# Redividing SBUF and the eight PSUM banks of an fp32r encoder kernel, and giving one more low part per product set to accumulating DMAs

## The chip, the cores and the metric

The kernel runs on one core of a Trainium2 chip. The metric is the device time of one execution in microseconds (us). Five compute queues matter below: PE (TensorE, matrix products), DVE (VectorE), ACT (ScalarE), POOL (GpSimd) and SP (SyncE, which here only starts DMAs). POOL also starts DMAs of its own, among them accumulating ones.

## The reference

The computation is a two-layer encoder on x of 512 tokens by 1024 features. Cut to what matters:

```python
for i in range(DEPTH):                       # DEPTH = 2, ALPHA = 4 ** 0.25
    x = layer_norm(ALPHA * x + 0.5 * swiglu(x, w_gate[i, 0], w_up[i, 0], w_down[i, 0]))
    y = mixer_ab(x) if i % 2 == 0 else mixer_c(x)   # attention of several kinds
    x = layer_norm(ALPHA * x + y)
    x = layer_norm(ALPHA * x + memory_attn(x, mem))  # 4 heads into 256 memory tokens
    x = layer_norm(ALPHA * x + 0.5 * swiglu(x, w_gate[i, 1], w_up[i, 1], w_down[i, 1]))

def swiglu(x, w_gate, w_up, w_down):         # hidden width 2816
    return (silu(x @ w_gate) * (x @ w_up)) @ w_down
```

`mixer_ab` is 8 dense heads with 2-D rotary (A) and 8 heads in a band of +-128 tokens with a sink logit (B). `mixer_c` is 16 heads of clamped neighbourhood attention with a learned bias, worked in 8 pairs.

## The kernel before

**Stages.** `run()` goes through FFN 0, mixer_ab, memory 0, FFN 1, FFN 2, mixer_c, memory 1, FFN 3. In the profiled execution the FFNs lie at about 0–370, 760–1100, 1100–1445 and 1840–2191 us, mixer_ab at 370–560, mixer_c at 1445–1680, and the two memory stages behind the mixers.

**Arithmetic.** Each fp32 operand is split into a high part (an ACT cast to fp32r) and a low part (raw minus high, a DVE subtract), and `mm3` makes three matmuls of them: high·high, high·low, low·high. `wide(raw, shape, added)` splits a 128x1024 weight tile. With `added`, no DVE instruction is used: ACT writes `-raw` in fp32r into the low tile, and a DMA from POOL's queue adds `raw` to it in place.

**FFN.** A Strassen-like scheme of 7 products (1 to 7) replaces 8. `hidden()` computes 512 hidden columns by the products 1, 2, 6, 5, 7, 3, 4 of 24 matmuls of 256 columns each, into three banks pa, pb, pc with copies of pa and pc in between (v, u, y); products 1, 2 and 4 take a block of the weights as it is, the others sums and differences of blocks that DVE makes. It is called 10 times per FFN, 40 in all. `ADDED` lists the products whose left low part comes by the accumulating DMA. `down_fast()` (DF) multiplies two hidden blocks with the down weights, again by 7 products of 12 matmuls (2 banks x 2 x 3): product 1 into two banks, then 6, 2, 5, 7, 3, 4. Each bank is evicted by a DVE SCALAR_TENSOR_TENSOR of 128x512 into x or into the slab u2. Product 2 goes on in product 1's banks and 3 in those of 5, 4 in those of 7, so product 2 cannot start before the evictions of product 1.

**Order.** `Graph.record` notes every instruction (which is why the profile gives line 141 for all of them), and `Graph.emit` schedules them itself by a table of costs: each engine takes the first ready instruction by program order. A tile of a tag is granted in program order out of that tag's buffers (`grant`): a later tile never passes an earlier one of its tag that still waits for a buffer. So the number of buffers of a tag sets how far ahead work can be moved, and every engine then runs what it was given strictly in order.

**Pools.** `slab` is 4 KB per partition (weights, their high and low parts), `t2` 2 KB (attention probabilities, temporary mixes), `x` the residual. The PSUM has 8 banks of 2 KB: tag `a` 3 (hidden, scores), `d` 2 (DF products 1, 2, 7, 4; projections, attention outputs) and `t` 3 (transposes; DF 6, 5, 3). Two tiles stand apart: `junk`, the unused output of the Square in `layer_norm`, and `band`, the mask of the band heads. In tile names the digits are running numbers.

## Time and profile before

| what | us |
|---|---|
| median of three runs | 2192.2 (2191.91 to 2193.2) |
| the profiled execution itself | 2192.96 |
| its span, first to last instruction | 2191.2 |
| PE busy | 2142.4 (98%) |
| DVE busy | 1756.9 (80%) |
| ACT busy | 1155.9 (53%) |
| POOL busy | 318.1 (15%) |

The span is 1.76 us shorter than the execution's time, and the execution's time is 0.76 above the median. "Busy" of PE counts overlapping matmuls as one stretch. The granted TensorE clock is 0.997 over the span. An "idle before" or a "wait" in the profile is a stretch in which an engine had nothing running, with what ended it. Timelines show the start, the duration and the engine of a run of like instructions, in which xN stands for N of them.

### The profile page before, as it was taken

What the parts mean: (1) busy time and instruction counts of PE and PEld (TensorE: products, weight loads), DVE (VectorE), ACT (ScalarE), POOL (GpSimd) and SP (SyncE); (2) the same over time, 40 slices, a digit from 0 to 9 for tenths busy, and PEclk for the clock granted to TensorE, in tenths of its full rate; (3) what the DMA queues carried; (4) which work ended last, traced back from release to release, by engine and by line L of the source; (5) the groups of instructions that cost most, each with busy time, mean ns of one, the idle gap of its engine ahead of it and who ended that gap; (6) DMA issues with size and microseconds to landing.
All of it is one profiled execution on the core that took longest, in us unless ns stands there. A gap on an engine that the chain in (4) does not pass through costs nothing.

```text
span 2191.2 us, 35698 instructions
## 1 busy us (share of the span) xinstructions
PE 2142.4 (98%) x14212; PEld 1959.0 (89%) x14212; DVE 1756.9 (80%) x2476; ACT 1155.9 (53%) x1754; POOL 318.1 (15%) x431
## 2 busy tenths in 40 slices
PE   8999999999999999999999999999999999999998
PEld 8899998778898899998999998998889988999997
DVE  6989987778855799999799999767777458999985
ACT  6555554466533455654565555445554335655552
POOL 0000202534000000002000002113420000000020
PEclk9999999999999999999999999999999999999999
DMA  6544463011533164555435554635555233454453
GB/s 178 152 119 135 135 181 125 0 30 52 163 104 116 58 187 120 139 141 146 144 93 140 144 154 131 182 95 152 140 159 158 92 106 87 131 149 132 127 148 95
DMA packets 190199, 276.12 MB, mean 126 GB/s; under 512 B 11216, under 2 KB 141904, under 8 KB 190032
## 3 DMA queue, kind: packets, MB, share of 16 engines
q1 hardware_dynamic: 175440, 221.40, 32.7%
q0 software_dynamic: 14592, 52.44, 12.3%
q8 instruction: 111, 1.82, 0.3%
q14 instruction: 56, 0.46, 0.1%
HBM read 217.17 MB, written 4.19 MB: 101 GB/s over the span
## 4 chain that ended last, share of the span: by engine, by line
PE 85%; DVE 11%; ACT 2%; issue 1%; POOL 1%; DMA 0%; POOLq 0%; ACTq 0%; DVEq 0%
PE a L141 48%; PE d L141 26%; PE t L141 10%; DVE slab L141 8%; DVE t L141 2%; ACT slab L141 1%; DMA slab<-slab 0%; POOL t L141 0%; DVE x L141 0%; ACT t L141 0%; POOL rms8y L141 0%; POOL rms2y L141 0%; POOL slab L141 0%; DVE xl L141 0%; DVE mn L141 0%
## 5 line engine op out<-in xcount | busy, mean ns | idle before, releaser
L141 DVE TENSOR_TENSOR slab<-slab,slab 128x1024 fp32r<-128x1024 f32 (+2 forms) x776 | 920.0, 1217 | 58.0 <-ACT slab L141 54.8
L141 ACT CAST slab<-slab 128x1024 fp32r<-128x1024 f32 (+1 forms) x616 | 609.9, 1021 | 296.4 <-DVE slab L141 184.2
L141 PE MATMUL d<-slab,slab 128*128 128x512 f32 (+2 forms) x2432 | 576.2, 384 | 15.8 <-DVE slab L141 11.7
L141 PE MATMUL a<-xh,slab 128*128 128x256 f32 (+1 forms) x2960 | 571.5, 290 | 1.8 <-ACT slab L141 1.4
L141 PE MATMUL a<-slab,slab 128*128 128x256 f32 (+2 forms) x4216 | 555.9, 288 | 8.4 <-ACT t L141 6.1
L141 PEld LDWEIGHTS a<-slab,slab 128*128 128x128 f32 x4216 | 527.6, 192 | 22.2 <-ACT t L141 8.4
L141 PEld LDWEIGHTS d<-slab,slab 128*128 128x128 f32 x2432 | 438.9, 188 | 103.6 <-DVE slab L141 17.3
L141 PEld LDWEIGHTS a<-xh,slab 128*128 128x128 f32 x2960 | 474.1, 192 | 13.5 <-ACT slab L141 3.1
L141 PE MATMUL a<-xl,slab 128*128 128x256 f32 (+1 forms) x1480 | 428.3, 290 | 0.0
L141 PEld LDWEIGHTS a<-xl,slab 128*128 128x128 f32 x1480 | 283.5, 192 | 4.3
L141 POOL DMA_DIRECT2D slab<-slab x80 | 69.3, 866 | 1065.1 <-ACT slab L141 725.5
L141 DVE SCALAR_TENSOR_TENSOR x<-d,x 128x512 f32<-128x512 f32 x216 | 148.2, 688 | 56.0 <-PE d L141 54.2
L141 ACT CAST slab<-t 128x512 fp32r<-128x512 f32 (+1 forms) x209 | 109.8, 564 | 89.3 <-PE t L141 64.4
L141 PE MATMUL t<-slab,slab 128*128 128x512 f32 (+1 forms) x648 | 151.3, 381 | 1.8 <-DVE slab L141 1.7
L141 PEld LDWEIGHTS t<-slab,slab 128*128 128x128 f32 x648 | 115.1, 188 | 28.8 <-DVE slab L141 4.4
L141 DVE TENSOR_TENSOR slab<-t,slab 128x512 fp32r<-128x512 f32 (+1 forms) x209 | 128.3, 647 | 14.2 <-ACT slab L141 13.5
L141 POOL TENSOR_TENSOR t<-t,l 128x256 f32<-128x256 f32 (+2 forms) x104 | 84.5, 831 | 351.5 <-DVE l L141 292.4
L141 DVE TENSOR_TENSOR t<-a,t 128x512 f32<-128x512 f32 (+1 forms) x121 | 83.4, 689 | 64.0 <-PE a L141 57.1
L141 ACT ACTIVATE t<-t 128x512 f32<-128x512 f32 x80 | 50.6, 633 | 147.5 <-DVE t L141 147.5
L141 ACT COPY t<-a 128x512 f32<-128x512 f32 x120 | 69.9, 586 | 83.3 <-PE a L141 82.6
L141 PE MATMUL a<-slab,xh 128*128 128x256 f32 (+1 forms) x432 | 98.5, 321 | 3.8 <-ACT slab L141 3.1
L141 ACT ACTIVATE slab<-slab 128x1024 fp32r<-128x1024 f32 x80 | 84.6, 1057 | 0.0
(109 smaller groups left out, 1898.6 us busy)
## 6 DMA issues: line engine op xcount, KB each, us to landing
slab<-ffn_w_gate SPq DMA_DIRECT2D x88, 512.0 KB
slab<-ffn_w_up SPq DMA_DIRECT2D x88, 512.0 KB
slab<-ffn_w_down SPq DMA_DIRECT2D x88, 512.0 KB
slab<-slab POOLq DMA_DIRECT2D x80, 512.0 KB, 5.7
slab<-mem_w_kv SPq DMA_DIRECT2D x32, 512.0 KB
slab<-c_w_in SPq DMA_DIRECT2D x24, 512.0 KB
slab<-t SPq DMA_DIRECT2D x96, 128.0 KB
slab<-mem_w_q SPq DMA_DIRECT2D x16, 512.0 KB
```

The lines of the kernel that those rows point to most:

```text
L141: op.call = lambda: fn(*args, **kw)
```

## The change

1. `ADDED` gains product 1: in each of the 40 `hidden()` calls a third low part comes by ACT and an accumulating DMA of 512 KB instead of a DVE subtract.
2. `t2` goes from 14 buffers of 2 KB to 8. `junk` (2 KB) becomes a t2 tile in each layer_norm, `band` (1.5 KB) a t2 tile that lives through mixer_ab. `slab` goes from 31 to 35 buffers (16 KB more).
3. The eight banks become two sets: `d` 3, and `u` 5 for what was `a` and `t`.
4. Small tiles have 6 buffers in place of 8.

```diff
-ADDED = (2, 4)
+ADDED = (1, 2, 4)
...
-    BUFS = {"t2": 14, "slab": 31, "a": 3, "d": 2, "t": 3}
+    BUFS = {"t2": 8, "slab": 35, "u": 5, "d": 3}
...
     def ps(self, tag):
-        return self.tile(self.psp, [P, 512], F32, tag)
-
-    def small(self, n, tag, bufs=8):
+        return self.tile(self.psp, [P, 512], F32, "d" if tag == "d" else "u")
+
+    def small(self, n, tag, bufs=6):
...
-        nc.scalar.activation(self.junk, x, AF.Square, bias=nmu, scale=1.0, accum_out=var)
+        nc.scalar.activation(self.t2(BF16, (P, D)), x, AF.Square, bias=nmu, scale=1.0, accum_out=var)
...
+        band = self.t2(F32)[:, :384]
+        nc.sync.dma_start(out=band, in_=a["band"])
         nsink = self.small(8, "nsink", 1)
```

The pools decide the order, so the diff doesn't show what moves. Three places follow; rows are instructions in an engine's own order, x2 two alike.

PE at the end of a group of FFN 1, before: d_1816 holds product 1 and then product 2 of down_fast, t_1818 and t_1819 product 6, t_1820 product 5, and a_1846 is product 1 of the next `hidden()`.

```order
L141 MATMUL t_1819<-slab_1797,slab_1796 128x512
L141 MATMUL t_1820<-slab_1804,slab_1803 128x512 x2
L141 MATMUL t_1820<-slab_1805,slab_1803 128x512
L141 MATMUL t_1820<-slab_1804,slab_1803 128x512
L141 MATMUL a_1846<-xh_80,slab_1830 128x256
L141 MATMUL a_1846<-xl_81,slab_1830 128x256
L141 MATMUL a_1846<-xh_80,slab_1830 128x256
L141 MATMUL a_1846<-xl_81,slab_1830 128x256
L141 MATMUL d_1816<-slab_1801,slab_1799 128x512
```

The same place after: d_1827 holds products 1 and 2, u_1829 and u_1830 product 6, u_1831 and u_1832 the two banks of product 5.

```order
L141 MATMUL u_1830<-slab_1808,slab_1807 128x512
L141 MATMUL u_1831<-slab_1815,slab_1814 128x512
L141 MATMUL u_1832<-slab_1815,slab_1814 128x512
L141 MATMUL u_1832<-slab_1816,slab_1814 128x512
L141 MATMUL u_1832<-slab_1815,slab_1814 128x512 x2
L141 MATMUL u_1832<-slab_1816,slab_1814 128x512
L141 MATMUL d_1827<-slab_1812,slab_1810 128x512
```

Ahead of product 2 now stand 5 of the 6 matmuls of product 5's second bank, which had no bank before, and the four matmuls of the next `hidden()` are gone from there: its product 1 begins only behind product 4 of down_fast.

DVE at that place, before, from the last mix of `hidden()` that reads PSUM (a_1779) to the evictions of product 1 (d_1816, d_1817).

```order
L141 TENSOR_TENSOR slab_1732<-a_1779,t_1704_1782 128x512
L141 TENSOR_TENSOR t_1717_1795<-t_1716_1794,slab_1731 128x512
L141 TENSOR_TENSOR t_1732_1810<-slab_1732,t_1717_1795 128x512
L141 TENSOR_TENSOR slab_1800<-slab_1732,slab_1799 128x1024
L141 TENSOR_TENSOR slab_1796<-t_1717_1795,slab_1796 128x512
L141 TENSOR_TENSOR slab_1803<-t_1716_1794,slab_1803 128x512
L141 TENSOR_TENSOR slab_1811<-t_1732_1810,slab_1811 128x512
L141 TENSOR_TENSOR slab_1813<-slab_1787,slab_1812 128x1024
L141 TENSOR_TENSOR slab_1815<-slab_1788,slab_1814 128x1024
L141 SCALAR_TENSOR_TENSOR slab_1613<-d_1816,slab_1613 128x512
L141 SCALAR_TENSOR_TENSOR slab_1613<-d_1817,slab_1613 128x512
```

The same place after, from the same mix (u_1790) to the evictions of d_1827 and d_1828.

```order
L141 TENSOR_TENSOR slab_1743<-u_1790,t_1715_1793 128x512
L141 TENSOR_TENSOR t_1728_1806<-t_1727_1805,slab_1742 128x512
L141 TENSOR_TENSOR slab_1814<-t_1727_1805,slab_1814 128x512
L141 TENSOR_TENSOR slab_1811<-slab_1743,slab_1810 128x1024
L141 TENSOR_TENSOR slab_1807<-t_1728_1806,slab_1807 128x512
L141 TENSOR_TENSOR t_1743_1821<-slab_1743,t_1728_1806 128x512
L141 TENSOR_TENSOR slab_1826<-slab_1799,slab_1825 128x1024
L141 TENSOR_TENSOR slab_1822<-t_1743_1821,slab_1822 128x512
L141 SCALAR_TENSOR_TENSOR slab_1624<-d_1827,slab_1624 128x512
L141 SCALAR_TENSOR_TENSOR slab_1624<-d_1828,slab_1624 128x512
```

One of the three 128x1024 subtracts no longer stands between the mix and the evictions; it is done further ahead.

ACT in the band heads of mixer_ab, before: `CAST slab<-t` is the high part of a head's turned probabilities, `CAST slab<-d` that of an attention output, `ACTIVATE t<-t,mn` the exponentials of the next head's four token tiles.

```order
L141 CAST slab_1055<-t_1054 128x384
L141 ACTIVATE t_981_1059,l_1061<-t_981_1059,mn_1060 128x257
L141 CAST slab_1057<-t_1056 128x256
L141 CAST slab_1108<-slab_1107 128x1024
L141 CAST slab_1074<-d_1048 128x512
L141 ACTIVATE t_985_1063,l_1065<-t_985_1063,mn_1064 128x385
L141 ACTIVATE t_989_1067,l_1069<-t_989_1067,mn_1068 128x385
L141 ACTIVATE t_993_1071,l_1073<-t_993_1071,mn_1072 128x257
```

The same place after.

```order
L141 CAST slab_1058<-u_1057 128x384
L141 CAST slab_1060<-u_1059 128x256
L141 ACTIVATE t_984_1062,l_1064<-t_984_1062,mn_1063 128x257
L141 ACTIVATE t_988_1066,l_1068<-t_988_1066,mn_1067 128x385
L141 CAST slab_1077<-d_1051 128x512
L141 ACTIVATE t_992_1070,l_1072<-t_992_1070,mn_1071 128x385
L141 ACTIVATE t_996_1074,l_1076<-t_996_1074,mn_1075 128x257
```

The first exponential of the next head now stands behind all of a head's casts of turned probabilities, since a t2 buffer comes free for it only then.

## Prediction

> **What bounds the kernel now.** I read the page first: busy times, then the chain of work that ended last (row 2: shares of the span by engine), then the stretches by stage, then PE's waits, then timelines of two stalls.

> ```profile
> PE 2142.4 (98%) x14212; PEld 1959.0 (89%) x14212; DVE 1756.9 (80%) x2476; ACT 1155.9 (53%) x1754; POOL 318.1 (15%) x431
> PE 85%; DVE 11%; ACT 2%; issue 1%; POOL 1%; DMA 0%; POOLq 0%; ACTq 0%; DVEq 0%
> ```

> PE is the bound, with DVE in the chain for a ninth of it. The change alters no matmul, so its gain can only come from the time in which PE waits. The stretches (window, length, busy us of each engine, then granted clock, DMA share and GB/s) say where that is:

> ```profile
> 50.00:85.00 35.00, 31.59 (x176) 26.28 (x176) 33.64 (x42) 18.60 (x23) 0.85 (x1) 1.00 0.43 114
> 85.00:370.00 285.00, 281.23 (x1955) 262.41 (x1955) 248.49 (x293) 156.96 (x195) 38.54 (x39) 1.00 0.52 143
> 408.00:560.00 152.00, 140.39 (x787) 116.39 (x786) 122.21 (x319) 98.48 (x240) 65.75 (x104) 1.00 0.17 42
> 760.00:1100.00 340.00, 335.76 (x2356) 314.13 (x2355) 300.32 (x352) 190.11 (x240) 31.42 (x31) 1.00 0.53 143
> 1100.00:1445.00 345.00, 342.04 (x2410) 320.37 (x2409) 305.81 (x358) 193.49 (x244) 39.72 (x46) 1.00 0.51 138
> 1445.00:1680.00 235.00, 233.68 (x1484) 209.85 (x1484) 168.93 (x351) 123.42 (x271) 65.12 (x122) 1.00 0.53 147
> 1840.00:2140.00 300.00, 296.22 (x2113) 278.89 (x2112) 271.65 (x305) 174.01 (x216) 30.51 (x29) 1.00 0.51 133
> 2140.00:2191.00 51.00, 40.33 (x251) 36.22 (x249) 27.88 (x45) 13.25 (x20) 2.21 (x4) 0.93 0.27 86
> ```

> PE's idle time, length minus busy: 3.8 + 4.2 + 3.0 + 3.8 = 14.8 us in the four long FFN stretches, 3.4 in 50–85 (FFN 0's first groups), 11.6 in mixer_ab, 1.3 in mixer_c, 10.7 in the tail. In the FFNs DVE is busy 87 to 91% (300.32 of 340), so there it is the near second. PE's waits by releaser (total us, times, longest), first for the whole span, then for mixer_ab alone (408–560):

> ```profile
> PE d L141 <- DVE slab L141: 11.7, 18, 1.4
> PE a L141 <- ACT t L141: 6.1, 6, 1.2
> ...
> PE t L141 <- DVE slab L141: 2.9, 3, 1.3
> PE a L141 <- DVE slab L141: 2.8, 8, 0.7
> ...
> PE a L141 <- DMA slab<-slab: 0.3, 1, 0.3
> ...
> PE d L141 <- DVE slab L141: 2.0, 3, 1.4
> PE a L141 <- ACT t L141: 0.9, 1, 0.9
> ```

> So outside mixer_ab 15 waits of PE's `d` banks for DVE make 9.7 us, and 5 of bank a for ACT 5.2: together 14.9, against 14.8 us idle in the four FFN stretches.

> **The d wait.** Timeline of FFN 1, end of a group; the first row is product 1 of down_fast, the last its product 2:

> ```profile
> 918.98 2.91 PE L141 MATMUL d<-slab,slab 128*128 128x512 f32 x12
> 919.37 0.68 DVE L141 TENSOR_TENSOR slab<-a,t 128x512 f32<-128x512 f32 x1
> ...
> 921.76 4.46 PE L141 MATMUL t<-slab,slab 128*128 128x512 f32 x18
> ...
> 922.65 1.05 ACT L141 CAST slab<-slab 128x1024 fp32r<-128x1024 f32 x1
> ...
> 924.24 2.35 DVE L141 TENSOR_TENSOR slab<-slab,slab 128x1024 fp32r<-128x1024 f32 x2
> ...
> 926.05 0.28 PE L141 MATMUL a<-xh,slab 128*128 128x256 f32 x1
> ...
> 926.40 0.28 PE L141 MATMUL a<-xl,slab 128*128 128x256 f32 x1
> 926.51 1.28 DVE L141 SCALAR_TENSOR_TENSOR slab<-d,slab 128x512 f32<-128x512 f32 x2
> ...
> 927.25 0.96 PE L141 MATMUL d<-slab,slab 128*128 128x512 f32 x3 [0.57 <-DVE slab L141]
> ```

> Product 1's banks were full at about 921.9, but DVE evicts them at 926.51, behind two 128x1024 subtracts at 924.24. PE runs out at 926.40 + 0.12 (four 256-wide matmuls start 0.12 apart) = 926.52 and starts again at 927.25. From start to start that costs 0.73, where the idle column says 0.57: 0.16 more each, because a matmul's shown time overlaps the next.

> *What it costs after.* By the changed order DVE has two such subtracts rather than three between the mix at 919.37 and the eviction: (926.51 - 924.24) / 2 = 1.14 us less. PE has five more 512-wide matmuls of product 5 ahead of product 2 (18 take 926.05 - 921.76 = 4.29, 0.238 each: 1.19 us) and loses the four small ones (926.52 - 926.05 = 0.47): 0.72 more cover. 1.14 + 0.72 - 0.73 = 1.1 us of slack. This is where the third `d` bank, the five `u` banks and product 1's DMA act together: without either the stall shrinks but stays. The 15 waits cost 9.7 + 15 x 0.16 = 12.1 us. Their longest anywhere is 1.4, more than half over my example's 0.57, and not every group has its order, so I take -10; ends 0 and -12.1.

> **The a wait.** FFN 0, hidden block 8:

> ```profile
> 270.50 7.44 DVE L141 TENSOR_TENSOR slab<-slab,slab 128x1024 fp32r<-128x1024 f32 x5
> 277.85 0.68 DVE L141 TENSOR_TENSOR t<-a,t 128x512 f32<-128x512 f32 x1
> ...
> 278.57 0.63 ACT L141 ACTIVATE t<-t 128x512 f32<-128x512 f32 x1
> 279.10 1.06 ACT L141 COPY t<-a 128x512 f32<-128x512 f32 x2
> 279.72 1.46 PE L141 MATMUL a<-slab,slab 128*128 128x256 f32 x10 [1.23 <-ACT t L141]
> ```

> Product 7 waits for the copy of its bank, which stands on ACT behind the silu, which waits for a mix on DVE behind five slab operations. After, two or three stand there, as product 1's subtract (1.2) is gone, and the copies stay in the same ACT order. It has to come 1.4 earlier (1.23 + 0.16). Four such waits and one more: 5.2 + 5 x 0.16 = 6.0; I take -4, ends 0 and -6.

> **What product 1 costs elsewhere.** The groups by shape, the POOL issue's minimum/median/maximum in ns, the landing of all DMAs of POOL's queue into slabs, and the queue's share:

> ```profile
> L141 DVE TENSOR_TENSOR slab<-slab,slab 128x1024 fp32r<-128x1024 f32 x496 | 607.7, 1243 | 50.6 <-ACT slab L141 50.4
> L141 ACT ACTIVATE slab<-slab 128x1024 fp32r<-128x1024 f32 x80 | 84.6, 1057 | 0.0
> L141 POOL DMA_DIRECT2D slab<-slab x80: 850/860/1033, 30.8 to 2133.5; - x80
> DMA to landing us min/median/max: 4.0/5.7/12.2
> q0 software_dynamic: 14592, 52.44, 12.3%
> ```

> Removed: 40 DVE subtracts x 1.243 = 50 us, DVE 80% to 78%. Added: 40 x 1.057 = 42 us on ACT (53 to 55%, 190.11 of 340 in the FFN, so there is room), 40 x 0.866 = 35 us on POOL (idle in the FFNs), and half as many accumulates again: about 12.3% x 40 x 0.5 MB / 52.44 MB = 5% of the DMA engines, whose share in the FFNs is 0.52. No queue nears its end: 0. The DMAs stand in POOL's queue ahead of the tensor_tensors that add u2 to x, which are few.

> What matters is whether the low part lands ahead of product 1. In the changed order its ACT instruction follows two casts behind the point of the CAST at 922.65 above; done, if nothing waits, by 922.65 + 1.05 + 1.05 + 1.06 = 925.8. With 0.87 for the issue and 5.7 to land: 932.4. Product 1 of the next hidden block starts only behind down_fast's 84 matmuls, 918.98 + 84 x 0.238 = 939.0. That is 6.6 us of room, 0.1 with the longest landing of 12.2. The 80 DMAs of products 2 and 4 held PE for 0.3 us in all. I count 0, with up to 3 us for FFN 0's first group, where 3.4 us are idle anyway. Without this cover, a landing 2 us late at 36 blocks would be +72; nothing in the rows comes near.

> [...]

> **mixer_ab and mixer_c.** t2 falls from 14 buffers to 8, of which band takes one through mixer_ab. Rows by shape in 408–560:

> ```profile
> L141 POOL TENSOR_TENSOR t<-t,l 128x384 f32<-128x384 f32 x16 | 14.9, 946 | 3.1 <-DVE l L141 3.0
> L141 ACT ACTIVATE t<-t,mn 128x385 f32<-128x385 f32 x16 | 9.8, 613 | 0.7 <-DVE l L141 0.7
> L141 DVE CUSTOM_DVE_ANT_0 t<-a,band,nsink 128x384 f32<-128x384 f32 x16 | 9.3, 612 | 0.0
> ```

> After, a band head's last two probability tiles get their buffers only when the head before has been transposed. From there to their own transposes: band operation 0.61, exponential 0.61, scaling on POOL 0.95 twice (it does them one after the other), and about 0.8 of small steps and hand-overs by my estimate: 4 us. Between lies, by my count of the changed order's rows, 5.5 us of PE work (the attention output and the next scores); the stretch has 140.39 / 16 = 8.8 us of PE per head. So there is slack of 1.5: 0 lost. Bounds: the whole chain uncovered is 8 heads x 4 = +32; the 11.6 us of idle gone is the other end. On the other side `d` 3 lets the output projection fill PE while a head waits, and five `u` banks let a fourth scores bank start. I take -3 of the 11.6, the d and a waits quoted above for this stretch (2.0 + 0.9).

> In mixer_c the pairs share 8 t2 tiles where an iteration uses 13, so a pair's bias can be fetched only when the pair before is transposed:

> ```profile
> t<-bias POOLq DMA_DIRECT2D x16, 128.0 KB, 3.2
> ```

> Seven pairs x 0 to 3.2 us: 0 to +22. Its stretch has 1.3 us idle now; the rows between leave the bias about as much time as it needs, so I take 0.3 per pair, +2.

> **Four more slabs, six small tiles, junk in t2:** slabs let loads start earlier; SP's loads gave no PE wait outside the first 50 us, so 0. `junk` is held for one ACT instruction per token tile in layer_norm, when few other t2 tiles are alive: 0. The start and the tail (10.7) depend on the same last layer_norm: 0.

> **Sum:** -10 - 4 - 3 + 2 = -15, and -2 of the 2.9 + 2.8 us of other waits for DVE's slab operations, as DVE has 50 us less to do: -17. The profiled execution's own time is 2192.96 (span 2191.2 + 1.76), 0.76 above the median of 2192.2: 2192.96 - 17 = 2176, against the median 2175.

> **Rivals.** (A) *t2 is too small*: in mixer_ab and mixer_c the probabilities' FIFO becomes the bound. For it: 14 buffers to 6 or 7; POOL's scaling is serial, and mixer_ab waits already. Against: 1.5 us of slack. From 1.5 us more of chain per head it starts to cost; at 2 us per band head and 1.5 per pair it gives 2176 + 3 (mixer_ab's gain gone) + 16 + 8.5 (10.5 in place of 2), about 2204; with mixer_c as forecast it passes 2192 from 1.6 us per head on. That is the slower side. Chance 0.10. (B) *The stalls only move*: in DF the eviction of a later product waits, as DVE still has 88% of its time, or product 1's low lands 2 us late in some 7 of the 40 blocks, which eats 14 of the 17. For it: DVE's share in the FFNs falls only by 3 points. Against: the slack of 1.1 and 6.6 above. Then 2185 to 2198, about 2190. Chance 0.14, half of it within 0.2%. (C) *More*: with free banks, mixer_ab's 11.6 us of idle goes by half as well and every FFN wait vanishes: 12.1 + 6 + 8 + 2 = 28, about 2165. Chance 0.12. (D) the forecast, 2168 to 2186: 0.64.

> **How the numbers follow.** 0.2% is 4.4 us, about what a measurement of this kernel can tell from no change: faster means under 2187.8, slower over 2196.6. Faster: D and C, and a third of B: 0.64 + 0.12 + 0.05 = 0.81. Same: 0.07 of B and 0.03 of A: 0.10. Slower: 0.09. The range leaves out most of A, some of B and of C: 2160 to 2191.

> **What would show it.** Right: no d wait of PE for DVE over 0.3 us in the FFNs, idle there under 6 us in the four stretches; the DVE subtract group with 456 of 496; 120 accumulates with a landing under 8 us median; mixer_ab's stretch no longer than 150. Wrong: PE waiting on the slab DMA at product 1, PE idle in 1445–1680 well over 1.3, or waits of DVE's band operation or of the bias for a t2 tile.

## The result and the profile after

| | us |
|---|---|
| before, median of 4 runs | 2192.27 (2191.91 to 2193.2) |
| after, median of 4 runs | 2159.77 (2158.54 to 2161.68) |
| ratio after / before | 0.9852, 95% interval 0.9835 to 0.9869 |
| profiled execution after, and its span | 2161.68, 2159.8 |

The change saves 32.5 us by the medians, 31.4 by the spans of the two profiled executions. The direction was forecast; the size was not: 17 were expected, and the time lies 0.2 us below the range.

The page after, busy times and the chain by engine:

```profile
PE 2130.8 (99%) x14212; PEld 1964.5 (91%) x14212; DVE 1704.2 (79%) x2436; ACT 1190.8 (55%) x1794; POOL 353.4 (16%) x471
PE 91%; DVE 5%; issue 1%; DMA 1%; POOL 1%; ACT 1%; POOLq 0%; DVEq 0%; ACTq 0%
```

DVE's share of the chain falls from 11% to 5%. PE has the same 14212 matmuls, yet its busy time falls by 11.6 us: part of a short wait is counted as busy, because a matmul's shown time reaches over the start of the next (at 256 columns 0.28 us are shown and the next starts 0.12 later, at 512 0.39 and 0.23). The stretches after, in the columns of before (later ones hold slightly other work, since everything has moved up):

```profile
50.00:85.00 35.00, 31.42 (x177) 27.58 (x176) 29.22 (x36) 17.34 (x22) 2.56 (x3) 0.95 0.59 151
85.00:370.00 285.00, 284.49 (x1976) 266.33 (x1976) 244.34 (x290) 166.98 (x206) 42.91 (x46) 1.00 0.60 161
408.00:560.00 152.00, 146.79 (x818) 124.84 (x819) 126.26 (x321) 100.47 (x243) 64.65 (x103) 0.99 0.23 64
760.00:1100.00 340.00, 339.43 (x2402) 319.91 (x2401) 293.89 (x347) 202.10 (x254) 40.88 (x42) 1.00 0.61 160
1100.00:1445.00 345.00, 344.22 (x2441) 324.43 (x2440) 290.90 (x346) 198.18 (x248) 46.79 (x49) 1.00 0.57 150
1445.00:1680.00 235.00, 235.00 (x1508) 213.26 (x1507) 167.03 (x357) 126.07 (x280) 62.99 (x126) 1.00 0.55 157
1840.00:2140.00 300.00, 299.23 (x2104) 281.74 (x2104) 253.53 (x293) 171.26 (x210) 36.78 (x36) 1.00 0.58 147
```

PE's idle time in the four long FFN stretches is 0.5 + 0.6 + 0.8 + 0.8 = 2.7 us where it was 14.8, and 0 in the mixer_c stretch. PE's waits over the whole span, in the columns of before:

```profile
PE u L141 <- ACT slab L141: 3.6, 2, 3.1
PE u L141 <- POOL slab L141: 3.2, 1, 3.2
PE u L141 <- DMA slab<-slab: 3.1, 1, 3.1
PE d L141 <- ACT slab L141: 2.6, 5, 0.5
PE u L141 <- ACT t L141: 2.3, 4, 0.9
PE d L141 <- DVE slab L141: 2.0, 3, 1.3
```

The d waits for DVE fall from 11.7 us (18) to 2.0 (3): the 15 outside mixer_ab are gone. New are single waits of 3 us: one for a low part by DMA, one for POOL. At the end of the group whose stall was shown before:

```profile
905.41 2.91 PE L141 MATMUL d<-slab,slab 128*128 128x512 f32 x12
905.80 0.68 DVE L141 TENSOR_TENSOR slab<-u,t 128x512 f32<-128x512 f32 x1
...
908.15 5.38 PE L141 MATMUL u<-slab,slab 128*128 128x512 f32 x23
...
911.68 1.28 DVE L141 SCALAR_TENSOR_TENSOR slab<-d,slab 128x512 f32<-128x512 f32 x2
```

From the mix to the eviction DVE takes 911.68 - 905.80 = 5.9 us, 926.51 - 919.37 = 7.1 before. Product 2's first matmul starts at 913.37, right behind the 23 matmuls of products 6 and 5. It needs only the first of the two evictions (before, it started at 927.25, while the second one ran until 927.79). That one ends at 912.37: no wait, and 1.0 us to spare.

**A measure for the comparisons.** Idle time undercounts waits, so I use *excess*: the sum, over PE's matmuls in order, of the start-to-start interval less the bare one of its width (0.109 us for 128 columns, 0.120 for 256, 0.174 for 384, 0.227 for 512, about 0.11 for the 64 matmuls of 192: the intervals of the undisturbed rows). All kernels here issue the same matmuls, 2112.2 us of bare intervals, so excess, put to the stage of the earlier matmul, adds up to the difference in PE's last start. "Start" is groups 0 and 1 of FFN 0, "blocks 1–3" the groups with down_fast elsewhere, "blocks 8–10" the FFNs' remaining hidden blocks, "tail" is from PE's last start to the end of the span. In us, from one profiled execution each:

| kernel | start | blocks 1–3 | blocks 8–10 | mixer_ab | memory | mixer_c | tail |
|---|---|---|---|---|---|---|---|
| before | 15.0 | 13.6 | 9.2 | 20.0 | 4.7 | 3.8 | 11.25 |
| only_added | 14.2 | 12.2 | 5.9 | 23.5 | 4.7 | 4.2 | 9.68 |
| only_banks | 13.4 | 1.8 | 24.4 | 11.9 | 0.4 | 2.4 | 11.32 |
| only_pools | 12.9 | 5.4 | 8.0 | 26.3 | 4.7 | 4.1 | 11.26 |
| all_but_added | 10.2 | 1.3 | 14.7 | 14.3 | 0.6 | 0.8 | 11.25 |
| all_but_banks | 14.3 | 1.7 | 3.1 | 26.2 | 4.8 | 4.3 | 9.69 |
| all_but_pools | 13.1 | 1.0 | 25.3 | 12.7 | 0.5 | 2.3 | 9.76 |
| after | 14.8 | 0.5 | 4.1 | 15.5 | 0.6 | 1.0 | 9.70 |
| products_2_4_5 | 9.4 | 0.6 | 15.1 | 15.4 | 0.6 | 0.9 | 9.98 |
| second_block_by_dve | 11.3 | 0.5 | 4.3 | 14.2 | 0.6 | 0.8 | 9.70 |
| u6_d2 | 13.1 | 1.4 | 3.2 | 18.8 | 3.8 | 2.3 | 9.69 |
| u4_d4 | 12.4 | 0.5 | 5.4 | 21.3 | 4.3 | 10.6 | 9.69 |
| t2_10_slab_34 | 11.5 | 0.5 | 3.9 | 10.5 | 0.6 | 6.5 | 9.69 |
| keys_earlier | 9.9 | 0.5 | 4.0 | 14.6 | 0.7 | 0.8 | 9.70 |

Before to after: -0.2, -13.1, -5.1, -4.5, -4.1, -2.8, -1.6, in all -31.4, the difference of the spans.

Each row also holds the stretches of 3.4 us in which PE ran at half rate in that execution (last section); one adds 1.4 to 1.9 us. In mixer_ab there is none in before, all_but_added, second_block_by_dve, t2_10_slab_34 and keys_earlier, two in only_pools, all_but_banks and all_but_pools, and one in each of the others. Blocks 8–10 hold three in only_banks, all_but_added and all_but_pools and two in products_2_4_5.

### The profile page after: what moved, and what is told of

Its sections match the earlier page's. It is cut to its first block, busy times and chain, and to the rows that moved or that the text cites. A ratio compares the mean times of both kernels' runs of the same rounds, so it can differ in the third digit from the quotient of the medians.

```text
span 2159.8 us, 35839 instructions
## 1 busy us (share of the span) xinstructions
PE 2130.8 (99%) x14212; PEld 1964.5 (91%) x14212; DVE 1704.2 (79%) x2436; ACT 1190.8 (55%) x1794; POOL 353.4 (16%) x471
## 4 chain that ended last, share of the span: by engine, by line
PE 91%; DVE 5%; issue 1%; DMA 1%; POOL 1%; ACT 1%; POOLq 0%; DVEq 0%; ACTq 0%
PE u L141 62%; PE d L141 28%; DVE slab L141 3%; DMA slab<-slab 1%; DVE t L141 1%; POOL x L141 0%; DVE x L141 0%; ACT slab L141 0%; DVE mn L141 0%; ACT t L141 0%; POOL slab L141 0%; POOL rms8y L141 0%; POOL rms2y L141 0%; DVE rms2y L141 0%; ACT L141 0%
## 5 line engine op out<-in xcount | busy, mean ns | idle before, releaser
L141 DVE TENSOR_TENSOR slab<-slab,slab 128x1024 fp32r<-128x1024 f32 (+2 forms) x736 | 868.1, 1214 | 45.8 <-ACT slab L141 41.4
L141 ACT CAST slab<-slab 128x1024 fp32r<-128x1024 f32 (+1 forms) x616 | 611.0, 1021 | 210.4 <-DVE slab L141 176.7
L141 PE MATMUL u<-slab,slab 128*128 128x256 f32 (+2 forms) x4864 | 696.7, 300 | 1.4 <-ACT t L141 1.4
L141 PEld LDWEIGHTS u<-slab,slab 128*128 128x128 f32 x4864 | 645.3, 191 | 34.4 <-ACT t L141 2.2
L141 PE MATMUL u<-xh,slab 128*128 128x256 f32 (+2 forms) x3072 | 605.5, 294 | 3.6 <-DMA slab<-slab 3.1
L141 PE MATMUL d<-slab,slab 128*128 128x512 f32 (+2 forms) x2432 | 572.5, 384 | 4.8 <-ACT slab L141 2.6
L141 PEld LDWEIGHTS d<-slab,slab 128*128 128x128 f32 x2432 | 441.9, 188 | 89.9 <-ACT slab L141 4.9
L141 PEld LDWEIGHTS u<-xh,slab 128*128 128x128 f32 x3072 | 494.1, 192 | 16.5 <-DMA slab<-slab 3.4
L141 PE MATMUL u<-xl,slab 128*128 128x256 f32 (+2 forms) x1536 | 451.5, 294 | 0.0
L141 PEld LDWEIGHTS u<-xl,slab 128*128 128x128 f32 x1536 | 294.5, 192 | 6.1
L141 POOL DMA_DIRECT2D slab<-slab x120 | 103.8, 865 | 985.7 <-ACT slab L141 557.0
L141 DVE SCALAR_TENSOR_TENSOR x<-d,x 128x512 f32<-128x512 f32 x216 | 147.5, 687 | 75.3 <-PE d L141 73.5
L141 DVE TENSOR_TENSOR t<-u,t 128x512 f32<-128x512 f32 (+1 forms) x128 | 88.2, 689 | 95.4 <-PE u L141 70.2
L141 ACT COPY t<-u 128x512 f32<-128x512 f32 x121 | 70.9, 586 | 138.1 <-PE u L141 137.9
L141 ACT CAST slab<-u 128x512 fp32r<-128x512 f32 (+3 forms) x161 | 77.6, 536 | 114.5 <-PE u L141 73.1
L141 POOL TENSOR_TENSOR t<-t,l 128x256 f32<-128x256 f32 (+2 forms) x104 | 87.2, 854 | 273.0 <-DVE l L141 268.5
L141 PE MATMUL u<-slab,xh 128*128 128x256 f32 (+1 forms) x576 | 124.7, 312 | 3.8 <-ACT slab L141 3.1
L141 ACT ACTIVATE slab<-slab 128x1024 fp32r<-128x1024 f32 x120 | 126.9, 1058 | 0.0
L141 DVE TENSOR_TENSOR slab<-u,slab 128x512 fp32r<-128x512 f32 (+3 forms) x161 | 91.7, 607 | 38.7 <-ACT slab L141 38.3
L141 ACT ACTIVATE t<-t 128x512 f32<-128x512 f32 x80 | 50.5, 632 | 108.4 <-DVE t L141 108.1
L141 PEld LDWEIGHTS u<-slab,xh 128*128 128x128 f32 x576 | 96.0, 195 | 9.6 <-ACT slab L141 3.4
L141 PE MATMUL u<-slab,xl 128*128 128x256 f32 (+1 forms) x288 | 89.8, 312 | 0.0
## 6 DMA issues: line engine op xcount, KB each, us to landing
slab<-t SPq DMA_DIRECT2D x96, 128.0 KB
```

What stands on the lines that cost most here:

```text
L141: op.call = lambda: fn(*args, **kw)
```

## The experiments

The change has three parts: product 1's low part by DMA ("added"), the bank sets ("banks"), the SBUF moves ("pools"). The first six kernels are all their other combinations; ratios are to the kernel before on the same chip.

| added | banks | pools | kernel | median us | ratio (95%) |
|---|---|---|---|---|---|
| x | | | only_added | 2191.9 | 0.9995 (0.9986–1.0005) |
| | x | | only_banks | 2181.7 | 0.9945 (0.9929–0.9962) |
| | | x | only_pools | 2187.8 | 0.9974 (0.9963–0.9985) |
| | x | x | all_but_added | 2168.8 | 0.9886 (0.9871–0.9900) |
| x | | x | all_but_banks | 2179.6 | 0.9938 (0.9923–0.9953) |
| x | x | | all_but_pools | 2181.6 | 0.9955 (0.9940–0.9970) |

**only_added.**

```diff
-ADDED = (2, 4)
+ADDED = (1, 2, 4)
```

> The kernel before with one edit: ADDED = (1, 2, 4), so 120 accumulating DMAs; pools and banks stay. Theory DVE (the change wins because DVE has 50 us less to do): the d waits of the FFNs (9.7 us idle, 12.1 from start to start) and the a waits (6.0) go, memory and the mixers stay as before: 2192 - 16 = 2176. Theory banks (the third d bank and the five u banks carry the gain): product 2 still has only 18 matmuls in front of it and the next hidden block's start stays early, so at most half of the FFN waits go, and that early start waits for a DMA that is not there yet: 2184 to 2200. Theory pools: about 2190, because 31 slabs are taken by product 1's longer life.

2191.9: no change that can be measured. DVE is busy 45.5 us less (1756.9 to 1711.4), which brings nothing by itself. The d waits are all there:

```profile
PE d L141 <- DVE slab L141: 11.0, 18, 1.4
```

So theory DVE falls as a theory of the whole. The excess of blocks 8–10 falls by 3.3 us, that of mixer_ab grows by 3.5: its first keys wait 3.0 us for POOL in place of 1.2, and a stretch at half rate follows.

**only_banks.**

```diff
-    BUFS = {"t2": 14, "slab": 31, "a": 3, "d": 2, "t": 3}
+    BUFS = {"t2": 14, "slab": 31, "u": 5, "d": 3}
...
-        return self.tile(self.psp, [P, 512], F32, tag)
+        return self.tile(self.psp, [P, 512], F32, "d" if tag == "d" else "u")
```

> The kernel before with one edit: tags a and t become u with 5 banks, d gets 3. Theory banks: memory loses its 2 x 2.0 us of excess, mixer_c 2.4, mixer_ab 4, the FFNs at least half of their 17, together about -20: 2172. Theory DVE: the FFN waits stay, the rest goes: 2192 - 10 = 2182. Theory pools: 2188 or more.

2181.7, nearer theory DVE's 2182 than theory banks' 2172, but not for its reason: the table shows blocks 1–3 clear (13.6 to 1.8) and mixer_ab, memory and mixer_c better by 8.1, 4.3 and 1.4, together 25.6. Blocks 8–10 give 15.2 back. Timeline of block 8 in FFN 2:

```profile
1330.31 13.17 DVE L141 TENSOR_TENSOR slab<-slab,slab 128x1024 f32<-128x1024 f32 x9
...
1334.30 2.77 PE L141 MATMUL u<-slab,slab 128*128 128x256 f32 x21 [2.32 <-DVE slab L141]
...
1335.33 1.77 POOL L141 DMA_DIRECT2D slab<-slab  x2
...
1337.66 3.02 PE L141 MATMUL u<-slab,slab 128*128 128x256 f32 x23 [0.59 <-DVE slab L141]
...
1343.12 0.70 PE L141 MATMUL u<-xh,slab 128*128 128x256 f32 x2 [2.44 <-DMA slab<-slab]
```

DVE does nine slab operations in a row, PE stands in front of them, and then in front of a low part whose DMA was issued only from 1335.33 on. I read it so that the waits of blocks 1–3 had become a queue that comes due at block 8, the prediction's rival B. Three stretches at half rate, one in each of three FFNs, are some 4.5 of the 24.4.

**only_pools.**

```diff
-    BUFS = {"t2": 14, "slab": 31, "a": 3, "d": 2, "t": 3}
+    BUFS = {"t2": 8, "slab": 35, "a": 3, "d": 2, "t": 3}
```

with `junk` and `band` as t2 tiles and 6 small tiles.

> The kernel before with the SBUF moves alone: t2 8, slab 35, junk and band as t2 tiles, 6 small tiles; ADDED and banks stay. Theory banks and theory DVE: nothing gained, and a loss of 0 to 10 us in the mixers where t2 is short: 2192 to 2202. Theory pools: loads start earlier, FFN 0's first groups and the mixers gain: 2180 to 2187.

2187.8, theory pools' upper edge plus 0.8. It is a gain and a loss: blocks 1–3 fall from 13.6 to 5.4, and mixer_ab grows by 6.3. I put the gain down to the four more slabs, which let low parts be made ahead of the evictions: they are the only part of the pools that adds room, but no run has them alone. The loss is not rival A's: the eight band heads go only from 5.3 to 6.0. It lies about the first keys and scores (+3.4) and at dense heads 5 to 7, where the next keys and values are turned (+3.4), and heads 0 to 4 give 1.4 back. In both places stands a single wait of over 2 us, and behind each a stretch at half rate that costs 1.7 and 1.9:

```profile
PE t L141 <- DVE slab L141: 2.2, 1, 2.2
...
PE t L141 <- POOL slab L141: 2.1, 1, 2.1
```

**all_but_added.** The changed kernel with `ADDED = (2, 4)`.

> The changed kernel with ADDED = (2, 4): banks and pools stay changed. Theory banks: within 6 us of the changed kernel's 2160, perhaps faster by the 4.5 us of excess that its first group of FFN 0 loses to the DMA of product 1: 2156 to 2166. Theory DVE: the FFN waits are back: 2174 to 2178.

2168.8, between the two. Banks and pools together save 24, more than their 11 + 5. What is missing to 2160 is block 8: 14.7 of excess against 4.1. PE's wait there in FFN 2 (1320–1375) is

```profile
PE u L141 <- DVE slab L141: 2.3, 1, 2.3
```

**all_but_banks and all_but_pools.** After these four I held that the banks make DVE what PE waits for, and that product 1's DMA pays only then.

> The changed kernel with the banks of before (a 3, d 2, t 3). Theory debt (the banks let PE run closer behind DVE, and product 1's DMA is worth something only where DVE has become what PE waits for): without the banks the DMA brings next to nothing, as alone, so about as the pools alone, 2184 to 2189. Theory sum (each part has its own gain): the changed kernel's 2160 plus the 11 that the banks brought alone, 2169 to 2173.

2179.6: both theories wrong. With the pools the DMA brings 8 us even without the new banks (2187.8 to 2179.6), most of it at blocks 1–3 (5.4 to 1.7) and 8–10 (8.0 to 3.1).

> The changed kernel with SBUF as before (t2 14, slab 31, junk and band apart, 8 small tiles). Theory debt: the banks' new waits at hidden block 8 (7.5, 2.7, 7.6 and 5.8 us of excess in the four FFNs) go with 50 us less work on DVE, the rest stays: 2182 - 18 = 2164, 2160 to 2169. Theory sum: 2182 - 1 = 2181, as the DMA brought 1 alone.

2181.6: wrong as well, and theory sum's 2181 comes out. Without the pools the DMA brings nothing next to the banks. Block 8 still waits, now for the DMA itself; over the whole span:

```profile
PE u L141 <- DMA slab<-slab: 12.0, 4, 3.7
PE u L141 <- DVE slab L141: 6.5, 6, 1.4
```

So what product 1's DMA needs is not the banks but the pools. My reading, which no run tests by itself, is that the slabs are what counts: with 31 the tiles that the DMA needs early find no room, and the wait only changes its name. With the pools the DMA is worth 8 us with the banks of before and 8 to 9 with the new ones (2168.8 to 2159.8; 8.4 when each is set against the kernel before on its own chip).

**products_2_4_5.** The changed kernel with another product given to the DMA.

```diff
-ADDED = (1, 2, 4)
+ADDED = (2, 4, 5)
```

> The changed kernel with ADDED = (2, 4, 5): the third low part by DMA is product 5's in place of product 1's, so DVE is relieved by as much, at another place. Theory debt (DVE's total counts): 2157 to 2163, and FFN 0's first wait for a DMA is gone. Theory place (product 1's subtract was in the way of the mixes and evictions at the block's start, and product 5's low part comes of a sum that DVE makes late, so it lands late): 2166 to 2176, with waits for slab DMAs.

2168.7 (ratio 0.9890, 0.9875–0.9904): theory place, the same time as without a third product. DVE is about as free as after, but block 8 waits for the new low part (whole span):

```profile
PE u L141 <- DMA slab<-slab: 11.6, 4, 3.8
```

DVE's busy time is 1709.6 here and 1704.2 after. Product 5's raw operand is a sum that DVE makes; product 1's is a block that comes from HBM and lies ready. Together with all_but_pools this shows that DVE's total isn't what counts, but whether the low part stands before its product.

**second_block_by_dve.** The one wait that product 1's DMA itself causes is in FFN 0, group 1.

```diff
+        self.calls = getattr(self, "calls", 0) + 1
-        left = {1: self.wide(w["11"], shape, 1 in ADDED)}
+        left = {1: self.wide(w["11"], shape, 1 in ADDED and self.calls != 2)}
```

> The changed kernel, but in the second hidden block of the program (FFN 0, group 1) product 1's low part is made by DVE again. It tells what the one wait for a slab DMA (3.1 us) costs: with the excess of that group, 4.5 us in all, of which 1.2 are slow matmuls right behind it. Theory: 2160 - 3 to - 4.5 = 2155 to 2157. Rival: DVE is late there instead, within 1 of 2160.

2157.66 (2156.83 to 2157.93; ratio 0.9838, 0.9823–0.9853): 2.1 less than after, a little short of the forecast. Start goes from 14.8 to 11.3. It is faster than both kernels.

**u6_d2 and u4_d4.** The changed kernel with the eight banks divided otherwise.

```diff
-    BUFS = {"t2": 8, "slab": 35, "u": 5, "d": 3}
+    BUFS = {"t2": 8, "slab": 35, "u": 6, "d": 2}      # and "u": 4, "d": 4
```

> The changed kernel with the banks as u 6, d 2. Theory third d bank (in the memory stages and at the mixers' ends the output projection waits for an attention output to leave one of two d banks, and the mixers' fillers use the third): memory's 2 x 2.0 us of excess are back, mixer_c's 2.4 and 6 to 10 in mixer_ab, the FFNs stay: 2160 + 13 = 2173, 2170 to 2177. Theory one big set (a and t sharing five banks made the gain): 2157 to 2163, with memory as in the changed kernel.

2167.4 (0.9879, 0.9865–0.9894), between the two. Memory's 3.2 of 4.1 us come back, mixer_c 1.3 and mixer_ab 3.3; the FFNs stay clear. So the third d bank carries memory and part of the mixers.

> The changed kernel with the banks as u 4, d 4. Theory third d bank: memory stays at 0.2 us of excess, mixer_ab within 4 of its 14.8, the FFNs the same: 2157 to 2165. Theory one big set: a hidden block has three accumulators and its transposes in four banks, so the FFNs' block-8 waits or mixer_ab's scores come back, 2166 to 2176.

2180.5 (0.9937, 0.9917–0.9958): a fourth bank for d costs about 20 us. mixer_c has 10.6 of excess, memory 4.3, mixer_ab 21.3. PE's largest waits over the whole span are now those of u for DVE, first for evictions into x:

```profile
PE u L141 <- DVE x L141: 7.0, 5, 2.3
PE u L141 <- DVE slab L141: 5.6, 7, 2.2
```

Both sets count: memory's waits appear with two d banks and with four u banks, and 5 and 3 is the best of the three.

**t2_10_slab_34.** second_block_by_dve with 4 KB moved back.

```diff
-    BUFS = {"t2": 8, "slab": 35, "u": 5, "d": 3}
+    BUFS = {"t2": 10, "slab": 34, "u": 5, "d": 3}
```

> The kernel in which DVE makes product 1's low part in the second hidden block (2157.7), with 4 KB moved back: t2 10, slab 34. If eight t2 tiles still cost mixer_ab something beside the new banks (12.1 of excess with 14 t2 tiles, 14.8 with 8): -1 to -3, 2155 to 2157, mixer_ab at 11 to 13. If the 35th slab is what clears the FFNs: the block-8 waits come back by 2 us or more in each FFN, 2163 to 2170.

2158.7 (0.9839, 0.9824–0.9853), 1 us above its base and by the ratio level with it. The excess of mixer_ab falls by 3.7, a little more than expected, and that of mixer_c grows by 5.7, which no theory had. Most of it is one wait of 3.1 us for a transfer from a t2 tile into a slab (1420–1660), and 1.8 us of half rate behind it:

```profile
PE u L141 <- DMA slab<-t: 3.1, 1, 3.1
```

The 34 slabs don't bring block 8's waits back. Why that transfer comes late with one slab less and two t2 tiles more is open.

**keys_earlier.** second_block_by_dve with another order of projections in mixer_ab.

```diff
-        for cg, t in ((0, 0), (0, 1), (0, 2), (1, 0), (0, 3), (1, 1), (1, 2), (1, 3)):
+        for cg, t in ((0, 0), (0, 1), (0, 2), (1, 0), (1, 1), (1, 2), (1, 3), (0, 3)):
```

> The kernel in which DVE makes product 1's low part in the second hidden block (2157.7), with one more edit in mixer_ab: the projection of the last queries (0, 3) comes after those of all keys, so 24 matmuls of 512 columns (5.4 us) stand between the last key projection and the transposes of the keys, which waited 3.2 us for POOL and were followed by six matmuls at half rate. Theory: the wait goes and the half-rate matmuls with it, since they followed every wait of over 3 us and none of under 2.7: -3.4 - 1.2, 2153 to 2155, mixer_ab's excess 13.4 to 9 or 10. Rival (the wait moves to the transposes of the last queries, whose chain through POOL is longer): 2156 to 2159, and no half-rate matmuls unless that wait is over 3 us.

2156.55 (2155.51 to 2157.61; 0.9831, 0.9815–0.9848), the rival: the wait shrinks from 3.2 to 1.7, and others of mixer_ab grow, so its excess stays (14.2 to 14.6). The profiled run's gain is in the start (11.3 to 9.9), which the edit doesn't touch. It is not told apart from its base, whose runs overlap. What the expectation says of half-rate matmuls was wrong on its face: its own base has a wait of 3.2 us with none behind it, and in only_pools they follow waits of 2.1 and 2.2 us (last section).

## Why the prediction was right or wrong

Two steps failed: the term of mixer_c, forecast as a loss of 2 and measured as a gain of 2.8, and the memory stages, which got no term and gained 4.1. The terms of the FFNs held.

*The d wait (-10; 0 to -12.1).* Right, a little low: blocks 1–3 lost 13.1. The place measured as worked out: no wait, 1.0 us of slack where 1.1 were computed, from 1.25 us less on DVE's side (computed 1.14) and 0.42 more cover on PE's (0.72). But the statement that the stall shrinks and stays without the third d bank or the DMA is wrong: the pools with the DMA clear it too (1.7), banks and pools without the DMA as well (1.3), and the pools alone take more than half of it. The slabs were priced at 0 because no load waited; by the reading above they decide how early DVE can make a low part. The term also held three waits that were not the FFNs' (see Memory).

*The a wait (-4; 0 to -6).* Right: blocks 8–10 lost 5.1. The DMA alone takes them from 9.2 to 5.9, with the pools to 3.1. The profile of before does not show that the new banks alone raise that place to 24.4; beside them it takes both other parts to reach 4.1.

*Product 1's DMA (0, up to 3 in FFN 0's first group).* Right. The issues kept their time, and one wait came, in FFN 0:

```profile
L141 POOL DMA_DIRECT2D slab<-slab x120: 850/859/1033, 26.1 to 2099.8; - x120
...
DMA to landing us min/median/max: 3.9/6.4/11.2
```

The median landing rose from 5.7 to 6.4 us, the longest fell from 12.2 to 11.2, against 6.6 us of room. With DVE 84 to 86% busy in the FFNs, 120 issues took as long as 80 did at 87 to 91% (850 to 1033 ns in both, median 859 against 860). In FFN 0 the wait ahead of group 1's product 1 took 3.1 us, and matmuls at half rate cost 1.6 more behind it; the start is 14.8 after, and 11.3 where DVE makes that one low part.

*mixer_ab (-3; +32 to -11.6).* The sum is near, -4.5, but by luck. The -3 were the d and a waits of this stretch, 2.0 and 0.9, and they are still there, most at other heads (400–560, after):

```profile
PE u L141 <- POOL slab L141: 3.2, 1, 3.2
PE d L141 <- DVE slab L141: 2.0, 3, 1.3
PE u L141 <- ACT t L141: 1.8, 2, 0.9
PE u L141 <- DVE slab L141: 0.5, 1, 0.5
```

What went are waits that no term named; the largest were these (408–560, before):

```profile
PE a L141 <- DVE slab L141: 2.2, 7, 0.4
PE d L141 <- DVE l L141: 1.5, 1, 1.5
```

By parts, the pools cost 6.3 with the old banks, of which 3.6 are half rate, and 2.4 with the new (11.9 to 14.3); the banks bring 8.1 to 12.0. For the band heads "0 lost" stood within 1 us. What failed is that I looked for the cost of eight t2 tiles there alone; it came at the first keys and at heads 5 to 7.

*mixer_c (+2; 0 to +22).* The step that failed most, by 4.8: it measured -2.8. The short t2 costs 0.3 there with the old banks (3.8 to 4.1); no bias came late. What I left out is that the third d bank and the five u banks serve this stage too: it loses 3.3 us with them (4.1 to 0.8).

*Memory (no term).* -4.1; with two d banks 3.2 of it is lost again (u6_d2). Its waits were in view (560–760, before):

```profile
PE d L141 <- DVE slab L141: 0.7, 2, 0.5
PE d L141 <- ACT slab L141: 0.2, 1, 0.2
```

After, that window has none. Idle time showed 0.9 us there; start to start the first memory stage held 2.4. The prediction had even counted three of these waits, as the FFNs': of the 15 d waits outside mixer_ab, 12 with 8.5 us lie in the four FFN stretches, and 0.7 and 0.5 us in the two memory stages. That 14.9 us of waits met 14.8 of idle was chance.

*Start and tail (0).* The start -0.2, by two that cancel: group 0 of FFN 0 lost 2.8 and group 1 grew by 2.6. The tail -1.6. In every kernel with a third product by DMA the tail is 9.7 to 10.0, in every one without 11.2 or 11.3. It is not the output's store, whose last packet lands 3.4 us behind DVE's last instruction before and after. The traces put it at the DRAIN that closes POOL's queue: 7.53 us before, until 2.2 us behind that packet, and 3.85 after, done ahead of it; 7.5 in every kernel without the third product, 3.5 to 3.9 in every one with it. Why it is shorter is open.

*The sum.* 17 forecast, 31.4 between the profiled executions: 4.8 of the miss are mixer_c, 4.1 memory, 2.2 the FFNs, 1.6 the tail, 1.5 mixer_ab, 0.2 the start. The last 1.1 to the medians' 32.5 are the two profiled executions' own places, 0.7 and 1.9 above their medians. I see one root in the mis-sized terms: a resource was priced only where the trace showed its biggest wait. Rival C, with 28 us, came nearest; it had 0.12. Its sum takes 8 for half of mixer_ab's 11.6; with 5.8 it is 26.

*Rivals A and B.* Of A only the stage is right (only_pools, +6.3 in mixer_ab), not the place or the pairs of mixer_c. B is what only_banks does (+15.2 in blocks 8–10); the pools and product 1's DMA together take it away again.

## What to carry to other kernels

Where buffers set how far a schedule can run ahead, price each freed or taken buffer in every stage that uses its tag, not only in the stage with the largest wait; idle time showed 0.9 of a stage's 2.4 us, so count start to start. Moving work from a near-bound engine to a DMA brought nothing here until the pools were changed, and then it mattered which operand: one that lies ready early. A part that alone changes nothing can be worth 8 us beside another, so test parts in pairs before dropping one.

## What the runs showed of the hardware

After some waits PE ran at half rate. In FFN 0 after the change, behind the wait for the low part, the granted clock is 0.50 and matmuls of 512 columns start every 0.427 us in place of 0.227:

```profile
77.45 0.80 PE L141 MATMUL u<-xh,slab 128*128 128x256 f32 x2 [3.15 <-DMA slab<-slab]
...
78.47 2.62 PE L141 MATMUL d<-slab,slab 128*128 128x512 f32 x6
...
78.40:80.40 2.00, 2.00 (x7) 1.61 (x6) 0.00 (x0) 0.00 (x0) 0.00 (x0) 0.50 1.05 210
```

That adds 1.6 us to the wait. In mixer_ab of the same run a wait of 3.2 us for POOL is followed by the same, but in second_block_by_dve a wait of 3.2 us at the same place is followed by full rate, and in only_pools two waits of 2.1 and 2.2 us were followed by half rate.

```profile
405.06:408.47 3.41, 0.38 (x3) 0.38 (x4) 2.53 (x11) 0.45 (x2) 2.11 (x4) 1.00 0.00 0
408.47:411.88 3.41, 3.41 (x13) 2.93 (x12) 2.53 (x10) 1.33 (x3) 2.02 (x4) 0.50 0.02 5
```

second_block_by_dve, where the wait falls into two pieces,

```profile
399.34:402.75 3.41, 2.14 (x11) 1.45 (x9) 2.64 (x10) 0.45 (x2) 2.05 (x4) 1.00 0.00 0
402.75:406.16 3.41, 1.50 (x11) 1.41 (x12) 2.58 (x10) 0.82 (x3) 2.10 (x4) 1.00 0.00 0
406.16:409.57 3.41, 3.32 (x16) 2.44 (x15) 3.09 (x10) 2.15 (x5) 1.66 (x3) 1.00 0.00 0
```

and only_pools

```profile
406.60:410.01 3.41, 1.34 (x12) 1.10 (x11) 2.58 (x10) 0.44 (x2) 2.11 (x4) 1.00 0.00 0
410.01:413.42 3.41, 3.41 (x10) 2.65 (x10) 2.59 (x10) 1.45 (x3) 2.15 (x3) 0.50 0.00 0
```

PE idles 3.0 us of a piece in the first, 1.3 and 1.9 in the second, 2.1 in the third. Over the 14 traces, between 20 and 2140 us, each of the 24 pieces with 1.92 us of idle or more is followed by a piece at half rate. Of the pieces at full rate with 1.80 or less none is, and between the two both occur. Before and after hold two of the 24 (3.07 and 3.03, both in after); their next largest idle, 1.46, is followed by full rate. So 2.1 us of idle in one piece of only_pools were followed by half rate, and a wait of 3.2 in second_block_by_dve, split into 1.3 and 1.9, was not.
